# A decoder layer on one core: the last gate summed on VectorE, the indexer issued within the last projection block

## Chip, core and metric

The kernel runs on one core of a Trainium2 chip, in one launch. The metric is the device time in microseconds, as a median over runs. The core's engines are TensorE (PE, its weight loads PEld), VectorE (DVE), ScalarE (ACT), GpSimd (POOL) and SyncE (SP); SyncE issues nearly all DMAs.

## What is computed

One layer for 256 tokens of width 2048, all in float32:

```
ada = silu(c) W_ada + b_ada -> sh1, sc1, gt1, sh2, sc2, gt2     # six vectors of 2048
h = RMSNorm(x) * (1 + sc1) + sh1
q, k, v, qi, ki, wi, p = split(h W_in)
A = attention(q, k, v) over the 64 keys per query with the highest indexer score
    score = sum over 16 heads of relu(qi . ki) * wi, causal
B = causal averages of p over windows 2, 4, 8, 16, minus p, a linear map per group, a scale
x = x + gt1 * (concat(A, B) W_out)
h2 = RMSNorm(x) * (1 + sc2) + sh2
top-1 of 4 expert groups, then top-2 of its 8 experts; SwiGLU experts of width 512
x = x + gt2 * experts(h2)
```

W_ada has 100 MB, the 32 experts 403 MB, W_in 30 MB and W_out 17 MB; every weight is read once.

## The kernel before

The work goes through in this order. `block_ada` and `block_scales` sum the first two modulation vectors, and `project` (line 459) multiplies by W_in, in five blocks of input rows (`BLOCKS`); the loop at line 518 runs over blocks and over the seven parts of the output (`PARTS`). Then come the pooling sums and the map of the pooled channels (lines 536 to 559), `indexer` (line 369: rope, scores, eight rounds of max and match-replace that mark the 64 best keys), `norm_qk`, `attend` (`probs` and `weigh`) and `out_proj` (line 601), once for the pooled half (`mixP`) and once for the attention half (`mixA`). `out_proj` calls a function after each of its four column tiles: `beside_pool` issues indexer, norms and attention there, `route_block` transposes the finished columns and multiplies them by the router's weights. Then the router's choice, and eight groups of four experts: `gather`, `hidden` (w1 and w3), `down` (w2), `combine`.

The other four modulation vectors are summed meanwhile in pieces of 128 input rows, 1 MB each. `fill(n)` issues the next n steps of `fill_steps`: gt1, sc2, sh2, each sixteen pieces on VectorE (line 161: acc = w * s + acc, one instruction of 128 x 2048) and a step that sums acc over the partitions on TensorE. `gate_end` spreads a gate over the partitions with four products; `vec_end` (line 282) turns a vector into columns with sixteen products of one column. gt2 has steps of its own, `gt2_steps`: sixteen pieces on TensorE, each four products side by side in column groups of the array (line 324), then `end`, with four products and four copies (lines 336 and 337). `FILLS` says how many steps stand behind each part of a projection block.

Weights go into rings of buffers: a ring of four for W_in and W_out (`wtile`), a ring of three for the pieces (`FILL_SLOTS`, with a fourth, `LATE_SLOTS`, once the indexer's tile is free). The experts use twelve buffers (`MOE_SLOTS`), and their first thirteen tiles (`FIRST_SLOTS`) are loaded ahead, as buffers of the earlier stages come free. The pieces' buffers are among them.

Each engine takes its instructions in order. That order isn't the order of the code: a scheduler moves instructions when the kernel is built, as far as dependences and buffers allow.

Of the kernel before, what the change touches and what calls it, by code (L numbers as in the profile page):

```python
# [44 lines left out]
C_ID, C_TRI, C_ROPE, C_ROPE2, C_IOTA, C_DG, C_FILL, C_SEL, C_END = 0, 128, 256, 352, 368, 400, 404, 406, 410  # L45
# [4 lines left out]
def shape_constants():  # L50
# [22 lines left out]
    for g in range(4):  # L73
        k[32 * g, C_SEL + g] = 1.0
# [6 lines left out]
def layer_kernel(ctx: ExitStack, tc: tile.TileContext, x, c, w_ada, b_ada, norm1_g, w_in, q_norm_g,  # L81
# [37 lines left out]
    def t2(shape=(P, 512)):  # L119
        return rot.tile(list(shape), F32, tag="t2", name="t2", bufs=4)  # L120
# [162 lines left out]
    def vec_end(acc, bias, gain, name):  # L283
        av = acc.rearrange("p (k q r) -> p k r q", q=P, r=RB)
        pt = bank([P, KC], "fl")
        for k in range(KC):
            nc.tensor.matmul(pt[:, k:k + 1], lhsT=av[:, k // RB, k % RB], rhs=ones[:, 0:1], start=True, stop=True)
        v = one.tile([P, KC], F32, name=name)
        if gain is None:
            nc.vector.tensor_add(v, pt, bias)  # L290
        else:
            nc.vector.scalar_tensor_tensor(v, pt, 1.0, bias, op0=ALU.add, op1=ALU.add)
            nc.vector.tensor_mul(v, v, gain)
        results[name] = v
# [3 lines left out]
    def fill_steps():  # L298
        v2 = lambda j: v2T[:, 4 * j:4 * j + 4].rearrange("p k r -> p (k r)")
        for name, sec in (("gt1", 2), ("sc2T", 4), ("sh2T", 3)):  # L300
            acc = biased(sec)
            yield from ada_pieces(sec, acc, fill_ring)
            if sec == 2:
                yield lambda: gate_end(acc, name)
            elif sec == 4:
                yield lambda: vec_end(acc, v2(2), v2(0), name)
            else:
                yield lambda: vec_end(acc, v2(1), None, name)


    def gt2_steps():
        gb = one.tile([P, 512], F32, tag="V2", name="gb")
        nc.gpsimd.memset(gb, 0.0)
        for g in range(4):
            nc.gpsimd.dma_start(gb[32 * g:32 * g + 1], b_ada[5 * D + g * 512:5 * D + (g + 1) * 512].unsqueeze(0))
        held = {}

        def piece(k):
            if k == 0:
                held["p"] = bank([P, 512], "fl")  # L320
            w = slot([P, D], fill_ring)
            nc.sync.dma_start(w, w_ada[k * P:(k + 1) * P, 5 * D:6 * D])
            for g in range(4):
# [4 lines left out]
        yield from [lambda k=k: piece(k) for k in range(KC)]  # L328

        def end():  # L330
            gs = t2()
            nc.vector.tensor_add(gs, held["p"], gb)
            gt = one.tile([P, D], F32, tag="gate", name="gt2")
            for n in range(4):
                pt = bank([P, 512], "fl")
                nc.tensor.matmul(pt, lhsT=kc[:, C_SEL + n:C_SEL + n + 1].to_broadcast([P, P]), rhs=gs, start=True, stop=True)
                nc.scalar.copy(gt[:, n * 512:(n + 1) * 512], pt)
            results["gt2"] = gt

        yield end  # L340

    steps = fill_steps()
    gates = gt2_steps()

    def fill(n, of=None):
        for _ in range(n):
            step = next(of or steps, None)
            if step is not None:
                step()
# [165 lines left out]

    PARTS = [("pool", 0), ("pool", 1), ("qi", 0), ("kw", 0), ("qkv", 0), ("qkv", 1), ("qkv", 2)]
    FILLS = {2: (0, 0, 1, 0, 1, 0, 1), 3: (0, 0, 1, 0, 1, 1, 1), 4: (2, 2, 2, 0, 2, 1, 1)}
    for b, (k0, nk) in enumerate(BLOCKS):
        block_scales(b)
        for k in range(k0, k0 + nk):  # L520
            h = hcols(k, slice(0, S))
            nc.scalar.activation(h, h, AF.Identity, scale=s1T[:, k:k + 1], bias=sh1T[:, k:k + 1])
        nxt = block_ada(b + 1) if b + 1 < len(BLOCKS) else []
        for pi, part in enumerate(PARTS):
# [11 lines left out]
    wpl = wtile([P, NG, 2, 256])  # L536
    nc.sync.dma_start(wpl, w_pool.rearrange("g (k p) d -> p g k d", p=P))
    mixP = one.tile([P, KC // 2, S], F32, tag="H1", name="mixP")
    wa = one.tile([P, 8, S], F32, tag="N0", name="wa")
    wb = one.tile([P, 8, S], F32, tag="N1", name="wb")  # L540
    src = ppT
    for lv, dst in enumerate((wa, wb, wa, wb)):
        c0, lag = 2 * lv, 1 << lv
        nc.vector.tensor_add(dst[:, c0:8, lag:S], src[:, c0:8, lag:S], src[:, c0:8, 0:S - lag])
        nc.vector.tensor_copy(dst[:, c0:8, 0:lag], src[:, c0:8, 0:lag])
        src = dst
    for g, dst in enumerate((wa, wb, wa, wb)):
        sl = slice(2 * g, 2 * g + 2)
        nc.vector.tensor_mul(dst[:, sl, 0:EDGE], dst[:, sl, 0:EDGE], edge[:, g][:, None, :].to_broadcast([P, 2, EDGE]))
        nc.vector.scalar_tensor_tensor(ppT[:, sl], dst[:, sl], 1.0 / POOL_WINDOWS[g], ppT[:, sl], op0=ALU.mult, op1=ALU.subtract)  # L550
    for g in range(NG):
        py = bank([P, 2, S], "mm")
        for dd in range(2):
            for k in range(2):
                nc.tensor.matmul(py[:, dd], lhsT=wpl[:, g, k, dd * P:(dd + 1) * P], rhs=ppT[:, g * 2 + k],
                                 start=(k == 0), stop=(k == 1))
        for dd in range(2):
            j = g * 2 + dd
            nc.scalar.activation(mixP[:, j], py[:, dd], AF.Copy, scale=plT[:, j:j + 1])
# [40 lines left out]
    def out_proj(mix, k0, label, after=None):  # L600
        for n in range(4):
# [17 lines left out]
            fill(3)  # L619
# [51 lines left out]
    def route_block(n):  # L671
# [265 lines left out]
    fill(100, gates)  # L937
    for q in range(NQ):
        a = hidden(q * QE, xg)
        held = gwT  # L940
# [39 lines left out]
```

## Time and profile before

| | us |
|---|---|
| median of 3 runs | 1446.32 |
| lowest, highest | 1444.52, 1446.98 |
| the profiled execution | 1448.13 |
| its span, first to last instruction | 1446.3 |
| TensorE busy in it | 1176.1 |
| VectorE busy | 415.2 |
| ScalarE busy | 98.2 |

All times of the trace are counted from the start of the span. Busy shares are no measure of what bounds the kernel by themselves: a transfer of 557 MB runs beside everything, and the stages have different limits. So the trace is read by stage below. A row of the timeline has the start, the time that the instructions took from the first to the last, the engine, the line, the operation, the tile that is written and those read, the shapes, the count, and in brackets the idle time ahead of it with what ended it. A float32 matmul of the code is two matmul instructions of the trace.

### The profile page before, as it was taken

Reading aid. Unit: us, or ns where it says so; the run is one execution under the profiler, and the core shown is the slowest. Engines: PE = TensorE matmul, PEld = TensorE weight load, DVE = VectorE, ACT = ScalarE, POOL = GpSimd, SP = SyncE. Lnnn points to the kernel's source line nnn. Section 1 sums busy time; section 2 is a strip of 40 time slices with the busy share of each in tenths; the row PEclk is TensorE's granted clock in tenths of the full one; section 3 lists DMA queues with packets and bytes.
Section 4 is the critical chain, followed back from the end, with each engine's and each line's share of the span. In section 5 each row is a group of like instructions: output and inputs, shape, how many; then the busy total and the mean of one; then the engine's idle time right before and its main releaser. Section 6 shows DMA issues by size and latency. Waiting matters only on the chain. (4 is left out here: it accounts for less than half of the span.)

```text
span 1446.3 us, 13177 instructions
## 1 busy us (share of the span) xinstructions
PE 1176.1 (81%) x5403; PEld 469.8 (32%) x5403; DVE 415.2 (29%) x709; ACT 98.2 (7%) x222; POOL 9.2 (1%) x14
## 2 busy tenths in 40 slices
PE   6889999994999868868878876886886778688666
PEld 4444654543446513213213211321321321132111
DVE  1476668689711401201200120120120012012002
ACT  3200001013521200000000000000000000000000
POOL 1000000000000000000000000000000000000000
PEclk9999999995998899989988998998998999999888
DMA  9999999998985299999999999999999999999997
GB/s 326 362 390 389 391 357 349 382 323 326 385 335 224 114 422 421 421 422 420 421 422 421 421 421 421 422 421 421 420 421 421 421 421 422 421 422 421 420 399 247
DMA packets 125560, 557.02 MB, mean 385 GB/s; under 512 B 15956, under 2 KB 30252, under 8 KB 69944
## 3 DMA queue, kind: packets, MB, share of 16 engines
q1 hardware_dynamic: 123712, 553.94, 95.8%
q10 hardware_dynamic: 1624, 2.18, 0.4%
q8 instruction: 44, 0.72, 0.2%
q14 instruction: 20, 0.16, 0.0%
q0 software_dynamic: 160, 0.02, 0.0%
HBM read 554.00 MB, written 2.10 MB: 384 GB/s over the span
## 5 line engine op out<-in xcount | busy, mean ns | idle before, releaser
L819 PE MATMUL mm<-w,xg 128*32 128x512 f32 x2048 | 395.1, 697 | 150.0 <-DMA w<-in_w_dram 149.9
L819 PEld LDWEIGHTS mm<-w,xg 128*32 128x32 f32 x2048 | 86.0, 124 | 446.0 <-DMA w<-in_w_dram 272.9
L857 PE MATMUL b<-w,t 128*32 128x512 f32 x896 | 194.8, 613 | 37.9 <-DMA w<-in_w_dram 32.4
L799 DVE TENSOR_SCALAR xg<-b,sc2T,sh2T 128x128 f32<-128x128 f32 x128 | 42.3, 404 | 464.6 <-PE b L795 464.6
L482 PE MATMUL mm<-w,hT 128*128 128x512 f32 (+1 forms) x320 | 128.8, 555 | 12.1 <-DMA w<-in_w_in_dram 10.1
L161 DVE SCALAR_TENSOR_TENSOR acc<-w,sT,acc 128x2048 f32<-128x2048 f32 x48 | 112.6, 2346 | 0.5 <-DMA w<-in_w_ada_dram 0.3
L857 PEld LDWEIGHTS b<-w,t 128*32 128x32 f32 x896 | 48.2, 111 | 179.8 <-issue 87.2
L838 DVE TENSOR_TENSOR t<-b,gt 128x512 f32<-128x512 f32 (+1 forms) x33 | 20.9, 671 | 244.0 <-PE b L857 218.8
L482 PEld LDWEIGHTS mm<-w,hT 128*128 128x128 f32 x320 | 57.7, 200 | 77.7 <-issue 66.2
L823 ACT ACTIVATE t<-mm 128x512 f32<-128x512 f32 x8 | 4.8, 597 | 897.3 <-PE mm L819 897.3
L795 PEld LDWEIGHTS b<-gq,x1c 128*128 128x128 f32 x512 | 60.7, 198 | 15.0 <-issue 10.1
L841 PE MATMUL mm<-t,gwT 128*128 128x512 f32 (+1 forms) x132 | 64.1, 618 | 1.5 <-DVE t L838 1.1
L795 PE MATMUL b<-gq,x1c 128*128 128x128 f32 x512 | 63.9, 285 | 1.2 <-DVE gq L785 1.2
L202 DVE SCALAR_TENSOR_TENSOR bacc<-w,sT,bacc 128x1024 f32<-128x1024 f32 x45 | 57.8, 1284 | 21.7 <-DMA w<-in_w_ada_dram 20.4
L611 PE MATMUL mm<-w,mixA 128*128 128x512 f32 x128 | 60.6, 620 | 1.8 <-ACT mixA L597 1.8
L492 PE MATMUL b<-hT,w 128*128 128x256 f32 x256 | 58.9, 388 | 1.9 <-DMA w<-in_w_in_dram 1.8
L611 PE MATMUL mm<-w,mixP 128*128 128x512 f32 x128 | 56.3, 595 | 0.0
L492 PEld LDWEIGHTS b<-hT,w 128*128 128x128 f32 x256 | 49.6, 195 | 14.0 <-issue 3.9
L843 DVE TENSOR_TENSOR xs<-xs,mm 128x512 f32<-128x512 f32 (+1 forms) x66 | 44.2, 670 | 21.1 <-PE mm L841 20.9
L841 PEld LDWEIGHTS mm<-t,gwT 128*128 128x128 f32 x132 | 21.8, 193 | 43.4 <-DVE xs L843 27.5
L611 PEld LDWEIGHTS mm<-w,mixA 128*128 128x128 f32 x128 | 24.2, 197 | 31.1 <-issue 28.0
L611 PEld LDWEIGHTS mm<-w,mixP 128*128 128x128 f32 x128 | 23.9, 190 | 29.0 <-issue 28.2
(211 smaller groups left out, 542.9 us busy)
## 6 DMA issues: line engine op xcount, KB each, us to landing
w<-in_w_dram SPq DMA_DIRECT2D x380, 1024.0 KB, 19.8
w<-in_w_ada_dram SPq DMA_DIRECT2D x64, 1024.0 KB, 7.5
w<-in_w_ada_dram SPq DMA_DIRECT2D x64, 512.0 KB, 9.4
w<-in_w_in_dram SPq DMA_DIRECT2D x21, 1024.0 KB, 10.5
w<-in_w_out_dram SPq DMA_DIRECT2D x16, 1024.0 KB, 7.0
w<-in_w_in_dram SPq DMA_DIRECT2D x14, 512.0 KB, 9.8
w<-in_w_dram SPq DMA_DIRECT2D x8, 512.0 KB, 12.7
xs<-in_x_dram SPq DMA_DIRECT2D x2, 1024.0 KB, 6.8
```

The costliest lines, as they stand in the source:

```text
L161: nc.vector.scalar_tensor_tensor(acc, w, sT[:, k:k + 1], acc, op0=ALU.mult, op1=ALU.add)
L202: nc.vector.scalar_tensor_tensor(acc, w[:, kk], sT[:, k:k + 1], acc, op0=ALU.mult, op1=ALU.add)
L482: nc.tensor.matmul(po[:, :width], lhsT=hcols(k0 + j, slice(i * P, (i + 1) * P)), rhs=w[:, j], start=(j == 0), stop=(j == nk - 1))
L492: nc.tensor.matmul(ppool[n][:, u], lhsT=w[:, j, u * P:(u + 1) * P], rhs=hcols(k, slice(0, S)), start=(k == 0 and u % 2 == 0), stop=(k == K ...
L611: nc.tensor.matmul(po, lhsT=mix[:, k, i * P:(i + 1) * P], rhs=ws[k // 4][:, k % 4], start=(k == 0), stop=(k == 7))
L795: nc.tensor.matmul(px[:, u], lhsT=x1c[i][:, k // RB, k % RB], rhs=gq[:, i].rearrange("p e s -> p (e s)"), start=(i == 0), stop=(i == NT - 1))
L799: nc.vector.tensor_scalar(xg[:, k], px[:, u], sc2T[:, k:k + 1], sh2T[:, k:k + 1], op0=ALU.mult, op1=ALU.add)
L819: nc.tensor.matmul(h[e * CAP:(e + 1) * CAP, :], lhsT=xg[:, k, e * CAP:(e + 1) * CAP], rhs=ws[e][:, r], start=(k == 0), stop=(k == KC - 1), ...
L838: nc.vector.tensor_mul(y[:, 0:m], py, gt2[:, c0:c0 + m])
L841: nc.tensor.matmul(pz[:, 0:m], lhsT=gwT[:, i], rhs=y[:, 0:m], start=True, stop=True)
L843: nc.vector.tensor_add(xv, xv, pz[:, 0:m])
L857: nc.tensor.matmul(py[n // 2][e * CAP:(e + 1) * CAP, (n % 2) * 512:(n % 2 + 1) * 512], lhsT=aT[:, f, e * CAP:(e + 1) * CAP], rhs=ws[e][:, ...
```

## The change

gt2 becomes the fourth entry of `fill_steps`, with the same sixteen pieces on VectorE and `gate_end`; `gt2_steps` and its constants go. `vec_end` sums acc with four products in column groups, copies the result on ScalarE, transposes it in four steps, and reads one column in 32. `FILLS` puts no step in block 2 and more in block 4. In the last block `indexer` and the pooling sums are issued after the part "kw"; norms stand ahead of the pooled output projection, and all of `attend` behind its first column tile. The steps behind the column tiles are 4, 4, 4, 4 in the pooled half and 9, 9 in the attention half, and what is left (six pieces and `gate_end`) stands behind the first group's `hidden`.

```diff
     def vec_end(acc, bias, gain, name):
-        av = acc.rearrange("p (k q r) -> p k r q", q=P, r=RB)
-        pt = bank([P, KC], "fl")
-        for k in range(KC):
-            nc.tensor.matmul(pt[:, k:k + 1], lhsT=av[:, k // RB, k % RB], rhs=ones[:, 0:1], start=True, stop=True)
+
+        pg = bank([P, 512], "fl")
+        for n in range(4):
+            nc.tensor.matmul(pg[32 * n:32 * (n + 1)], lhsT=ones[:, 0:32], rhs=acc[:, n * 512:(n + 1) * 512],
+                             start=True, stop=True, skip_group_check=True, tile_position=(0, 32 * n))
+        gs = t2()
+        nc.scalar.copy(gs, pg)
+        pt = bank([P, RB, P], "fl")
+        for q in range(RB):
+            nc.tensor.transpose(pt[:, q], gs.rearrange("p (q r) -> p r q", r=RB)[:, q], ident)
+        sums = pt.rearrange("p r (k m) -> p k r m", m=32)[:, :, :, 0]
...
-        for name, sec in (("gt1", 2), ("sc2T", 4), ("sh2T", 3)):
+        for name, sec in (("gt1", 2), ("sc2T", 4), ("sh2T", 3), ("gt2", 5)):
             acc = biased(sec)
             yield from ada_pieces(sec, acc, fill_ring)
-            if sec == 2:
+            if sec in (2, 5):
                 yield lambda: gate_end(acc, name)
...
-    def gt2_steps():
...
-            for g in range(4):
-                nc.tensor.matmul(held["p"][32 * g:32 * (g + 1)], lhsT=sT[:, k:k + 1].to_broadcast([P, 32]),
-                                 rhs=w[:, g * 512:(g + 1) * 512], start=(k == 0), stop=(k == KC - 1),
-                                 skip_group_check=True, tile_position=(0, 32 * g))
...
+    def pool_sums():
...
+    def pool_map():
...
-    FILLS = {2: (0, 0, 1, 0, 1, 0, 1), 3: (0, 0, 1, 0, 1, 1, 1), 4: (2, 2, 2, 0, 2, 1, 1)}
+    FILLS = {3: (0, 0, 0, 0, 1, 1, 1), 4: (4, 4, 4, 3, 3, 3, 3)}
...
+            if last and part[0] == "kw":
+                indexer()
+                pool_sums()
...
+    mixP = pool_map()
...
             if after is not None:
                 after(n)
-            fill(3)
...
-    stages = [indexer, norm_qk, attend]
-
     def beside_pool(n):
-        if n < len(stages):
-            stages[n]()
+        if n == 0:
+            attend()
+            fill_ring[:] = LATE_SLOTS
+        fill(4)
 
     while "gt1" not in results:
         fill(1)
+    norm_qk()
     out_proj(mixP, 8, "wo_pool", beside_pool)
-    fill(14)
-    fill_ring[:] = LATE_SLOTS
...
-        if n < 3:
-            while n >= 1 and "sh2T" not in results:
-                fill(1)
-            if n == 2:
-                route_bias()
-            fill(6, gates)
+        if n < 2:
+            fill(9)
+        if n == 2:
+            route_bias()
...
     xg, gwT = gather(0)
-    fill(100, gates)
     for q in range(NQ):
         a = hidden(q * QE, xg)
+        if q == 0:
+            fill(100)
```

`pool_sums` and `pool_map` hold the pooling lines as they stood, in two functions.

The orders show three places. On VectorE, from the last sums of the projection (`pqkv`) on: `score` is the indexer's, `t` and `xs` belong to the pooled output projection. Before:

```order
L477 TENSOR_TENSOR pqkv<-pqkv,mm 128x512 x2
L161 SCALAR_TENSOR_TENSOR acc<-w,sT,acc 128x2048 x3
L615 TENSOR_TENSOR t_1074<-mm,gt_988 128x512
L616 TENSOR_TENSOR xs<-xs,t_1074 128x512
L161 SCALAR_TENSOR_TENSOR acc<-w,sT,acc 128x2048
L615 TENSOR_TENSOR t_1086<-mm,gt_988 128x512
L381 COPY t_1107<-pidx 128x128
```

And in the changed kernel:

```order
L386 TENSOR_SCALAR score<-r_1003,wis 128x128
L450 TENSOR_TENSOR pqkv<-pqkv,mm 128x512
L388 SCALAR_TENSOR_TENSOR score<-r_1003,wis,score 128x128
L159 SCALAR_TENSOR_TENSOR acc<-w,sT,acc 128x2048
L388 SCALAR_TENSOR_TENSOR score<-r_1003,wis,score 128x128
L450 TENSOR_TENSOR pqkv<-pqkv,mm 128x512
L388 SCALAR_TENSOR_TENSOR score<-r_1003,wis,score 128x128
```

The scores now begin among the projection's last sums; before, eight output products of the pooled half (`t`, `xs`) began ahead of them.

On TensorE, in the third column tile of the attention output projection (`mixA`); `fl` is written by the modulation sums, `sm` by the router's products. Before:

```order
L676 MATMUL b_1955<-kc,xs 128x128 x4
L324 MATMUL fl<-w,sT 32x512 x16
L611 MATMUL mm<-w,mixA 128x512 x2
L676 MATMUL b_1955<-kc,xs 128x128 x4
L611 MATMUL mm<-w,mixA 128x512 x6
L287 MATMUL fl<-ones,acc 128x1 x16
L683 MATMUL sm<-ws_1692,r_1964 128x36 x8
L611 MATMUL mm<-w,mixA 128x512 x3
L336 MATMUL fl<-t_2025,kc 128x512
```

And in the changed kernel, where the vector's sum stands a column tile earlier:

```order
L593 MATMUL mm<-w,mixA 128x512 x14
L285 MATMUL fl<-acc,ones 32x512 x4
L593 MATMUL mm<-w,mixA 128x512 x10
L656 MATMUL b_1719<-kc,xs 128x128 x4
L291 MATMUL fl<-kc,t_1773 128x128 x4
L593 MATMUL mm<-w,mixA 128x512
```

The gate's pieces (L324) and its spreading (L336) are gone from here, and the sixteen one-column products (L287) have become L285 and L291.

On SyncE, the first group's weights (L792 up, L831 down) with the six late pieces (L158), in the changed kernel; before, this stretch held expert tiles alone:

```order
L792 DMA w<-in_w_dram 128x2048 x8
L158 DMA w<-in_w_ada_dram 128x2048
L792 DMA w<-in_w_dram 128x2048 x11
L831 DMA w<-in_w_dram 128x2048
L158 DMA w<-in_w_ada_dram 128x2048 x3
L831 DMA w<-in_w_dram 128x2048 x8
L158 DMA w<-in_w_ada_dram 128x2048 x2
L831 DMA w<-in_w_dram 128x2048 x7
```

On VectorE five of the six sums follow in a row there, where before nothing stood between the first group's product and the second group's input (`xg`):

```order
L802 TENSOR_TENSOR t_2316<-t_2316,mm 128x512
L782 COPY gwT<-sm 128x256
L159 SCALAR_TENSOR_TENSOR acc<-w,sT,acc 128x2048
L810 COPY t_2417<-sm 128x512
L159 SCALAR_TENSOR_TENSOR acc<-w,sT,acc 128x2048 x5
L777 TENSOR_SCALAR xg<-b_2357,sc2T,sh2T 128x128 x8
L777 TENSOR_SCALAR xg<-b_2382,sc2T,sh2T 128x128 x8
```

So the second group's input has moved behind the last of the late pieces.

## Rows read from the trace of the kernel before

**Rows 1.** The page, 40 slices of 36.2 us: busy tenths of DMA, and GB/s.

```profile
DMA  9999999998985299999999999999999999999997
GB/s 326 362 390 389 391 357 349 382 323 326 385 335 224 114 422 421 421 422 420 421 422 421 421 421 421 422 421 421 420 421 421 421 421 422 421 422 421 420 399 247
```

**Rows 2.** Stages: length, busy us (count) by engine, clock, DMA share, GB/s.

```profile
0.00:221.70 221.70, 194.76 (x714) 112.47 (x715) 120.54 (x125) 26.55 (x42) 4.95 (x8) 0.96 1.01 366
221.70:262.00 40.30, 40.30 (x126) 19.70 (x127) 35.05 (x55) 4.36 (x9) 1.81 (x1) 1.00 0.95 364
262.00:382.70 120.70, 99.75 (x376) 55.27 (x374) 99.88 (x184) 34.73 (x119) 2.44 (x5) 0.86 0.92 348
382.70:496.50 113.80, 107.92 (x460) 65.33 (x460) 33.45 (x78) 27.74 (x47) 0.00 (x0) 0.91 0.64 250
496.50:501.00 4.50, 4.50 (x45) 1.46 (x48) 4.12 (x13) 0.00 (x0) 0.00 (x0) 1.00 0.01 4
501.00:1446.30 945.30, 728.87 (x3692) 215.55 (x3682) 122.18 (x258) 4.78 (x8) 0.00 (x0) 0.92 1.00 413
```

**Rows 3.** VectorE: first pooling sum, last softmax reciprocal, the page's group of piece sums.

```profile
221.72 2.28 DVE L544 TENSOR_TENSOR wa<-ppT 128x2040 f32<-128x2040 f32 x1 [6.50 <-ACT ppT L495]
...
382.56 0.17 DVE L581 RECIPROCAL sm<-sm 128x4 f32<-128x4 f32 x1
...
L161 DVE SCALAR_TENSOR_TENSOR acc<-w,sT,acc 128x2048 f32<-128x2048 f32 x48 | 112.6, 2346 | 0.5 <-DMA w<-in_w_ada_dram 0.3
```

**Rows 4.** VectorE's waits, 221.7 to 382.7: total us, times, longest.

```profile
DVE t L615 <- PE mm L611: 11.7, 4, 6.0
...
DVE pqkv L477 <- PE mm L482: 5.2, 4, 2.7
...
DVE r L573 <- PE b L570: 3.0, 2, 1.6
```

**Rows 5.** TensorE's timeline after 382.7, and the first expert product.

```profile
389.09 9.68 PE L611 MATMUL mm<-w,mixA 128*128 128x512 f32 x22
...
401.75 2.78 PE L324 MATMUL fl<-w,sT 128*32 128x512 f32 x24
...
433.31 1.87 PE L683 MATMUL sm<-ws,r 128*128 128x36 f32 x16
...
437.38 3.64 PE L324 MATMUL fl<-w,sT 128*32 128x512 f32 x32
...
448.39 7.40 PE L287 MATMUL fl<-ones,acc 128*128 128x1 f32 x32
455.65 3.61 PE L683 MATMUL sm<-ws,r 128*128 128x36 f32 x16
459.06 5.35 PE L611 MATMUL mm<-w,mixA 128*128 128x512 f32 x6
464.25 1.02 PE L336 MATMUL fl<-t,kc 128*128 128x512 f32 x2
...
496.51 12.29 PE L819 MATMUL mm<-w,xg 128*32 128x512 f32 x102
```

**Rows 6.** Windows of 4 us, columns as in rows 2.

```profile
452.00:456.00 4.00, 4.00 (x19) 4.00 (x18) 0.17 (x1) 0.00 (x0) 0.00 (x0) 0.74 0.01 4
...
460.00:464.00 4.00, 4.00 (x6) 1.69 (x5) 0.00 (x0) 0.00 (x0) 0.00 (x0) 0.50 0.00 0
...
480.00:484.00 4.00, 0.82 (x4) 0.85 (x5) 2.58 (x18) 2.41 (x4) 0.00 (x0) 0.65 0.00 0
484.00:488.00 4.00, 2.80 (x13) 2.67 (x14) 1.96 (x10) 0.07 (x1) 0.00 (x0) 0.50 0.02 4
```

**Rows 7.** TensorE and VectorE from the first group's up products to its down products.

```profile
545.96 1.04 PE L819 MATMUL mm<-w,xg 128*32 128x512 f32 x2 [1.35 <-DMA w<-in_w_dram]
...
561.70 6.71 PE L857 MATMUL b<-w,t 128*32 128x512 f32 x40 [0.78 <-DVE t L832]
...
551.03 2.64 DVE L799 TENSOR_SCALAR xg<-b,sc2T,sh2T 128x128 f32<-128x128 f32 x8 [50.34 <-PE b L795]
```

More of the change, by code (lines that the diff above doesn't have):

```diff
@@ L283, in vec_end @@
     def vec_end(acc, bias, gain, name):
[L284 to L287 removed]
+        pg = bank([P, 512], "fl")
[8 more added lines that the diff above has]
+        sums = pt.rearrange("p r (k m) -> p k r m", m=32)[:, :, :, 0]
         v = one.tile([P, KC], F32, name=name)
+        vv = v.rearrange("p (k r) -> p k r", r=RB)
         if gain is None:
[L290 removed]
+            nc.vector.tensor_add(vv, sums, bias)
         else:
[L292 to L293 removed]
+            nc.vector.scalar_tensor_tensor(vv, sums, 1.0, bias, op0=ALU.add, op1=ALU.add)
+            nc.vector.tensor_mul(vv, vv, gain)
         results[name] = v
@@ L308, in fill_steps, with fill @@
                 yield lambda: vec_end(acc, v2(1), None, name)
-    def gt2_steps():
[L312 to L323, printed above, removed]
-                nc.tensor.matmul(held["p"][32 * g:32 * (g + 1)], lhsT=sT[:, k:k + 1].to_broadcast([P, 32]),
-                                 rhs=w[:, g * 512:(g + 1) * 512], start=(k == 0), stop=(k == KC - 1),
-                                 skip_group_check=True, tile_position=(0, 32 * g))
[L328 to L340, printed above, removed]
     steps = fill_steps()
-    gates = gt2_steps()
-    def fill(n, of=None):
+    def fill(n):
         for _ in range(n):
-            step = next(of or steps, None)
+            step = next(steps, None)
             if step is not None:
@@ L514, in project @@
                 plain(pidx[:, i, 1024:1104], w, 80, i)
+    def pool_sums():
+        wa = one.tile([P, 8, S], F32, tag="N0", name="wa")
+        wb = one.tile([P, 8, S], F32, tag="N1", name="wb")
+        src = ppT
+        for lv, dst in enumerate((wa, wb, wa, wb)):
+            c0, lag = 2 * lv, 1 << lv
+            nc.vector.tensor_add(dst[:, c0:8, lag:S], src[:, c0:8, lag:S], src[:, c0:8, 0:S - lag])
+            nc.vector.tensor_copy(dst[:, c0:8, 0:lag], src[:, c0:8, 0:lag])
+            src = dst
+        for g, dst in enumerate((wa, wb, wa, wb)):
+            sl = slice(2 * g, 2 * g + 2)
+            nc.vector.tensor_mul(dst[:, sl, 0:EDGE], dst[:, sl, 0:EDGE], edge[:, g][:, None, :].to_broadcast([P, 2, EDGE]))
+            nc.vector.scalar_tensor_tensor(ppT[:, sl], dst[:, sl], 1.0 / POOL_WINDOWS[g], ppT[:, sl], op0=ALU.mult, op1=ALU.subtract)
+    def pool_map():
+        wpl = wtile([P, NG, 2, 256])
+        nc.sync.dma_start(wpl, w_pool.rearrange("g (k p) d -> p g k d", p=P))
+        mixP = one.tile([P, KC // 2, S], F32, tag="H1", name="mixP")
+        for g in range(NG):
+            py = bank([P, 2, S], "mm")
+            for dd in range(2):
+                for k in range(2):
+                    nc.tensor.matmul(py[:, dd], lhsT=wpl[:, g, k, dd * P:(dd + 1) * P], rhs=ppT[:, g * 2 + k],
+                                     start=(k == 0), stop=(k == 1))
+            for dd in range(2):
+                j = g * 2 + dd
+                nc.scalar.activation(mixP[:, j], py[:, dd], AF.Copy, scale=plT[:, j:j + 1])
+        return mixP
     PARTS = [("pool", 0), ("pool", 1), ("qi", 0), ("kw", 0), ("qkv", 0), ("qkv", 1), ("qkv", 2)]
-    FILLS = {2: (0, 0, 1, 0, 1, 0, 1), 3: (0, 0, 1, 0, 1, 1, 1), 4: (2, 2, 2, 0, 2, 1, 1)}
+    FILLS = {3: (0, 0, 0, 0, 1, 1, 1), 4: (4, 4, 4, 3, 3, 3, 3)}
     for b, (k0, nk) in enumerate(BLOCKS):
@@ L523, in layer_kernel @@
         nxt = block_ada(b + 1) if b + 1 < len(BLOCKS) else []
+        last = b + 1 == len(BLOCKS)
         for pi, part in enumerate(PARTS):
@@ L533, in layer_kernel @@
             piece()
[L536 to L559, printed above, removed]
+    mixP = pool_map()
     REP = NH // NKV
```

5 lines of the change are left out of this document (2 added, 3 removed).

## The prediction

> **What bounds the kernel now.** I read the slices first [rows 1]: the DMA engines are 90% busy or more in most slices and move 420 GB/s from slice 15 to the end, but slices 11 to 14 sink to 114 GB/s. The table by stage [rows 2] puts a figure on it. From 501 us on the transfers run at a share of 1.00 for 945.3 us: the expert weights are the bound there, and nothing but bytes shortens that stage. Between 382.7 and 496.5 the share is 0.64, and from 496.5 to 501 it is 0.01. So the time is the moment at which expert weights begin to flow without a pause, plus the 945.3 us that they then need. That moment is set by the first expert product: it starts at 496.51 [rows 5], and only its reads free the buffers that already hold weights. What sets the end is therefore the chain up to 496.51, not the transfers.
>
> That chain has two halves. Up to 382.7 VectorE leads: it does the pooling, the top-64 search, the norms, the softmax, and the running sums of the modulation pieces, and the last softmax reciprocal comes at 382.56 [rows 3]. It is busy 35.05 of the 40.3 us from 221.7 and 99.88 of the next 120.7 [rows 2]: 134.9 of 161.0 us. From 382.7 TensorE leads, busy 107.9 of 113.8 us [rows 2]: the attention half of the output projection, the router, the gather.
>
> **The change part by part.**
>
> *Indexer and attention earlier.* VectorE's order holds the same operations between the first pooling sum and the last softmax reciprocal, except that 28 running sums stand there in place of 29. The work is thus 134.9 minus one sum of 2.35 [rows 3], 132.6 us; with no idle time at all the mark would come at 221.7 + 132.6 = 354. Of the 26.1 us of idle time, 11.7 are waits for products of the pooled output projection [rows 4]: VectorE then has nothing else queued. In the new order scoring, search and norms stand between these, so I let them go. The waits for the last projection products (5.2) and for the attention scores (3.0) [rows 4] have no new cover; I keep these 8 us. The mark falls at 362, 20.7 us earlier. The ends are 354 (no idle) and 376 (all but 4 us of the idle time stays). I take 362 because the largest wait is the one whose place is filled. The projection before it doesn't move: on SyncE's queue 20 modulation pieces stand ahead of the last projection weight in both orders, and the scoring products that TensorE now does among the projection's are moved, not added. The memset and bias load that GpSimd gains run beside all this, far from any wait.
>
> *Last gate on VectorE instead of TensorE.* It takes sixteen steps of four column-group products off TensorE. Ten of these lie after 382.7, in four runs of 80 instructions, the first 24 in 2.78 us and the last 32 in 3.64 [rows 5]; with the two between (1.06 and 1.92) 9.4 us, on a stretch where TensorE is full. Of the four products that spread the gate, the first stands in that stretch (1.02 us [rows 5]) and three among the router's last steps, where I credit 1 us: 2 in all. On VectorE ten of the sixteen sums now come before the experts, 10 x 2.35 = 23.5 us; they go behind the mark of 362, where VectorE is busy only 33.45 of 113.8 us [rows 2]. If that cover were gone they would cost their 23.5.
>
> *Vectors summed in column groups.* Sixteen one-column products (32 instructions, 7.40 us at 448.39 [rows 5]) become four column-group products and four transposes. At 24 in 2.78 the first are 0.93 us for eight instructions; the transposes are at most 0.44 each (22 instructions in 9.68 [rows 5]): under 2.7 together. The ScalarE copy between lies behind other products. I take 5.5 saved, between 4.7 and 6. [...] The router products there take 3.61 us where the same sixteen took 1.87, and six instructions take 5.35 where 0.44 each would give 2.6 [rows 5]: 1.7 + 2.7 = 4.4 us. I expect them back.
>
> [...]
>
> *The stretch after the mark.* It was 113.8 us. Less 9.4, 2, 5.5 and 4.4 it is 92.5. Against that, TensorE in the new order has only eight attention output products ahead of the last softmax; before, 22 instructions of them (9.68 us at 389.09) bridged the wait for ScalarE's scaling and copies. I add 5 us of waiting, take off 3.5 for the four products more that are already done (8 x 0.44), and add 3 for a half clock after the pause, as it is seen at 480 to 488 after one [rows 6]. The stretch is 97 us, between 93 (no wait, no half clock) and 103 (twice of both). The first expert product then starts at 362 + 97 = 459, 37.5 us earlier.
>
> *Late pieces.* Six of the gate's pieces now load among the first experts. Each is 1.05 MB; at 421 GB/s [rows 1] that is 2.49 us, 14.9 together, added to the 945.3. Besides, VectorE's order puts five of these sums ahead of the second group's gathered input, and TensorE's order puts the gate's products ahead of the first down projection. Before, that went without a pause: last tile's product at 545.96, down projection at 561.70 [rows 7]. Now the last piece is fourteen tiles behind the last up-projection tile, about 35 us. Behind it come the sum (2.35) and the two conversions (2.64 each [rows 7]): 7.6 us in which three tiles still load. Then the first four tiles must be read, 32 instructions at 6.71/40 us [rows 7], 5.4, before a buffer comes free, and the next load takes up to a tile's 2.49 to run. The transfers pause for about 7.6 + 5.4 + 2.5 - 7.5 = 8 us, from 0 (the order of landing is kinder) to 14 (half clock).
>
> **The sum.** -20.7 (mark) - 16.8 (stretch) + 14.9 (bytes) + 8 (pause) = -14.6 us. The profiled execution took 1448.13 us with a span of 1446.3, so it is 1.8 over the median of 1446.32; I take the difference from the trace and apply it to the median: 1432.
>
> **The rivals.**
>
> *VectorE's chain does not come earlier (slower).* VectorE takes its queue in order, and 28 sums of 2.35 us, 66 of the 132.6 us, stand inside the chain of scores, search and softmax. Each must wait for its own megabyte, in a ring of three buffers, and the output weights share the queue. If the pieces land late, the mark stays at 382.7: 20.7 us are gone and the bytes and the pause remain, 1432 + 20.7 = 1452. It decides from a mark at 376.5. For it speaks that VectorE has only 26.1 us of idle time before the mark, less than the search and the sums can be shifted about in. Against it: all 48 sums together waited 0.5 us, 0.3 of them for DMA [rows 3].
>
> *The gain is larger.* No idle time before the mark (354), a stretch of 94 us, and no pause: -28.7 - 19.8 + 14.9 = -33.6, 1413. For it: VectorE's waits have single causes [rows 4]. Against it: the products that feed it are themselves in a full TensorE queue.
>
> *The late pieces hold the experts up.* The two last pieces need buffers that come free only after sums that stand behind the first group's own product. If that puts the pieces one behind the other, the pause is about 20 instead of 8: 1444, no change to be told.
>
> *The half clock stays.* If it is not the one-column products that bring it but the short router products around them, which the change keeps, the 4.4 us stay: 1436. For it speaks that the router's own products run in the same windows; against it, that the clock was still full where such products ran alone (1.87 us for sixteen at 433.31 [rows 5]). [...]
>
> **How the numbers follow.** Forecast 1432: 0.50. Larger gain, 1413: 0.20. Half clock stays, 1436: 0.06. Late pieces, 1444: 0.12, a third of it still below the bound. VectorE's chain, 1452: 0.12. What a measurement of this kernel can tell from no change is 0.2%, 2.9 us, so faster is below 1443.4: 0.50 + 0.20 + 0.06 + 0.04 = 0.80; the same 0.08; slower 0.12. The range goes from 1414, at the larger gain, to 1446, which leaves out the slower case and the best tail.
>
> **What would show it.** In the changed kernel the last softmax reciprocal should stand near 362 and the first expert product near 459; the DMA share should be near 0 for some 15 us before the experts instead of 20, and dip once for 5 to 10 us at the first down projection; no half clock behind the vector sums; from there a share of 1.00 for about 960 us. The forecast is wrong in its first step if the mark stands later than 370, in its second if the first expert product is more than 103 us behind the mark, in its third if the experts' stage is longer than 945.3 + 15 + 14.

## The result

The changed kernel takes 1425.84 us (median of four runs, 1424.56 to 1427.49) where the kernel before took 1446.17 beside it: a ratio of 0.9861 (0.9844 to 0.9879), 20.3 us less. The forecast was 1432. In the two profiled executions the difference is larger, 1448.13 to 1424.56, 23.6 us, because the one of before lies 2.0 above its median and the one of after 1.3 below its own. The sum of the steps is held against these 23.6.

The slices of the changed kernel's page (35.6 us each), to be laid beside [rows 1]: one slice is weak, the 13th, where the 13th and 14th were, and a new dent stands in the 16th.

```profile
DMA  9999998999992998999999999999999999999998
GB/s 325 357 386 387 399 373 339 357 369 366 375 385 113 422 422 335 421 422 421 422 422 421 421 422 421 421 421 421 422 420 422 421 421 422 421 421 421 420 405 282
```

The stages, cut at the same marks as in [rows 2]: first pooling sum, last softmax reciprocal, first expert product, transfers running again. The columns are those of [rows 2].

```profile
222.93:262.00 39.07, 39.07 (x137) 18.62 (x138) 35.63 (x65) 5.98 (x13) 1.81 (x1) 1.00 0.92 344
262.00:359.67 97.67, 90.67 (x296) 46.74 (x294) 95.60 (x174) 32.91 (x111) 2.29 (x2) 0.98 0.97 368
359.67:452.10 92.43, 86.41 (x353) 55.28 (x353) 54.20 (x85) 26.09 (x46) 0.00 (x0) 0.89 0.74 295
452.10:457.00 4.90, 4.90 (x49) 1.58 (x52) 4.11 (x13) 0.00 (x0) 0.00 (x0) 1.00 0.17 25
457.00:1422.70 965.70, 724.92 (x3698) 213.79 (x3686) 136.04 (x264) 8.41 (x13) 0.00 (x0) 0.92 1.00 412
```

VectorE is now busy 131.2 of the 136.7 us up to the mark, where it was busy 134.9 of 161.0. The mark, and VectorE's waits up to it (total, times, longest), which answer [rows 3] and [rows 4]:

```profile
359.67 0.18 DVE L563 RECIPROCAL sm<-sm 128x4 f32<-128x4 f32 x1 [0.71 <-ACT r L562]
```

```profile
DVE wa L496 <- ACT ppT L468: 4.1, 1, 4.1
DVE kiT L358 <- PE sm L357: 2.9, 1, 2.9
DVE sm L563 <- ACT r L562: 1.5, 2, 0.8
DVE pqkv L450 <- PE mm L455: 0.3, 1, 0.3
```

The first of these waits lies just ahead of the first pooling sum, so outside the stretch. Of the 11.7 us for pooled output products nothing is left.

TensorE behind the mark, as in [rows 5] (L573 turns the attention weights, L593 is the output projection, L285 and L291 the vector's sum, L647 the router's bias, L663 the router, L797 the experts):

```profile
360.08 4.24 PE L573 MATMUL b<-kc,r 128*128 128x128 f32 x16 [2.58 <-ACT r L565]
...
380.67 1.06 PE L285 MATMUL fl<-acc,ones 128*32 128x512 f32 x8
381.67 8.85 PE L593 MATMUL mm<-w,mixA 128*128 128x512 f32 x20
...
390.82 0.65 PE L291 MATMUL fl<-kc,t 128*128 128x128 f32 x4
...
426.93 4.97 PE L647 MATMUL sm<-wr,sh2T 128*128 128x36 f32 x32
432.28 3.60 PE L663 MATMUL sm<-ws,r 128*128 128x36 f32 x16 [0.38 <-DVE brt L649]
...
452.10 12.01 PE L797 MATMUL mm<-w,xg 128*32 128x512 f32 x102
```

And the dent: windows of 4 us (as in [rows 6]) around the first down projection, then the rows of VectorE, TensorE and SyncE from the timeline that belong to it (as in [rows 7]).

```profile
544.00:548.00 4.00, 1.67 (x2) 0.50 (x2) 3.96 (x7) 0.00 (x0) 0.00 (x0) 0.50 1.01 420
548.00:552.00 4.00, 3.40 (x7) 0.69 (x6) 3.50 (x11) 0.59 (x1) 0.00 (x0) 0.50 0.34 139
552.00:556.00 4.00, 4.00 (x34) 0.99 (x32) 0.00 (x0) 0.59 (x1) 0.00 (x0) 1.00 0.02 4
556.00:560.00 4.00, 4.00 (x34) 1.23 (x34) 0.00 (x0) 0.59 (x1) 0.00 (x0) 1.00 0.90 330
```

```profile
541.44 4.83 DVE L159 SCALAR_TENSOR_TENSOR acc<-w,sT,acc 128x2048 f32<-128x2048 f32 x2 [13.49 <-DMA w<-in_w_ada_dram]
...
546.33 2.08 PE L277 MATMUL fl<-acc,ones 128*128 128x512 f32 x2 [27.56 <-DVE acc L159]
...
521.51 2.81 SPq L158 DMA_DIRECT2D w<-in_w_ada_dram  x2
```

The last two pieces are issued at 521.51, when their buffers come free, and are summed from 541.44; VectorE waits 13.49 us for them and TensorE 27.56 for the sum. By then the expert buffers are full: SyncE waits 11.1 us for a down product before it can issue the next load. From 549 to 556 hardly anything is moved, and 7.0 us are lost in these windows (4 us times what each lacks to 1).

Three terms make the difference between the profiled executions: the mark 382.56 to 359.67, -22.9; mark to first expert product 113.95 to 92.43, -21.5; from there to the end of the span 949.8 to 970.6, +20.8. Together -23.6.

### The profile page after: what moved, and what is told of

It reads as the page before. It is cut to its first block, busy times and chain, and to the rows that moved or that the text cites. A ratio compares the mean times of both kernels' runs of the same rounds, so it can differ in the third digit from the quotient of the medians.

```text
span 1422.7 us, 12863 instructions
## 1 busy us (share of the span) xinstructions
PE 1136.9 (80%) x5235; PEld 446.8 (31%) x5235; DVE 448.2 (32%) x724; ACT 99.9 (7%) x224; POOL 9.0 (1%) x11
## 5 line engine op out<-in xcount | busy, mean ns | idle before, releaser
L797 PE MATMUL mm<-w,xg 128*32 128x512 f32 x2048 | 392.3, 684 | 158.2 <-DMA w<-in_w_dram 158.0
L797 PEld LDWEIGHTS mm<-w,xg 128*32 128x32 f32 x2048 | 84.9, 122 | 449.3 <-DMA w<-in_w_dram 275.8
L835 PE MATMUL b<-w,t 128*32 128x512 f32 x896 | 187.9, 600 | 33.8 <-DMA w<-in_w_dram 28.4
L159 DVE SCALAR_TENSOR_TENSOR acc<-w,sT,acc 128x2048 f32<-128x2048 f32 x64 | 150.2, 2347 | 14.5 <-DMA w<-in_w_ada_dram 13.8
L455 PE MATMUL mm<-w,hT 128*128 128x512 f32 (+1 forms) x320 | 128.9, 555 | 15.2 <-DMA w<-in_w_in_dram 11.6
L773 PEld LDWEIGHTS b<-gq,x1c 128*128 128x128 f32 x512 | 60.2, 196 | 18.1 <-issue 11.7
L593 PE MATMUL mm<-w,mixA 128*128 128x512 f32 x128 | 56.7, 594 | 0.7 <-ACT mixA L579 0.7
L593 PE MATMUL mm<-w,mixP 128*128 128x512 f32 x128 | 56.1, 594 | 0.4 <-DVE t L597 0.4
L802 DVE TENSOR_TENSOR t<-t,mm 128x512 f32<-128x512 f32 x8 | 5.5, 687 | 139.5 <-PE mm L797 139.5
L593 PEld LDWEIGHTS mm<-w,mixP 128*128 128x128 f32 x128 | 24.0, 190 | 29.9 <-issue 27.3
## 6 DMA issues: line engine op xcount, KB each, us to landing
w<-in_w_dram SPq DMA_DIRECT2D x380, 1024.0 KB, 19.8
```

The costliest lines, as they stand in the source:

```text
L159: nc.vector.scalar_tensor_tensor(acc, w, sT[:, k:k + 1], acc, op0=ALU.mult, op1=ALU.add)
L455: nc.tensor.matmul(po[:, :width], lhsT=hcols(k0 + j, slice(i * P, (i + 1) * P)), rhs=w[:, j], start=(j == 0), stop=(j == nk - 1))
L593: nc.tensor.matmul(po, lhsT=mix[:, k, i * P:(i + 1) * P], rhs=ws[k // 4][:, k % 4], start=(k == 0), stop=(k == 7))
L773: nc.tensor.matmul(px[:, u], lhsT=x1c[i][:, k // RB, k % RB], rhs=gq[:, i].rearrange("p e s -> p (e s)"), start=(i == 0), stop=(i == NT - 1))
L797: nc.tensor.matmul(h[e * CAP:(e + 1) * CAP, :], lhsT=xg[:, k, e * CAP:(e + 1) * CAP], rhs=ws[e][:, r], start=(k == 0), stop=(k == KC - 1), ...
L835: nc.tensor.matmul(py[n // 2][e * CAP:(e + 1) * CAP, (n % 2) * 512:(n % 2 + 1) * 512], lhsT=aT[:, f, e * CAP:(e + 1) * CAP], rhs=ws[e][:, ...
```

## The experiments

Each was timed beside the kernel before on its chip (medians of 1444.6 to 1446.9). The table gathers the three marks of every profiled execution; each row's experiment follows. The profiled execution lies 7.6 us above the median in e3, 3.8 in e2 and 1.5 in e5, so the marks of these three rows can't be set against the medians beside them.

| kernel | median us | ratio to before | last softmax reciprocal | first expert product | from it to the end |
|---|---|---|---|---|---|
| before | 1446.17 | 1 | 382.56 | 496.51 | 949.8 |
| changed | 1425.84 | 0.9861 (0.9844 to 0.9879) | 359.67 | 452.10 | 970.6 |
| e1 | 1476.07 | 1.021 (1.0191 to 1.0228) | 412.25 | 498.20 | 974.8 |
| e2 | 1438.74 | 0.9944 (0.9926 to 0.9962) | 366.61 | 467.25 | 973.6 |
| e3 | 1439.95 | 0.9957 (0.9942 to 0.9973) | 358.53 | 460.84 | 984.8 |
| e4 | 1407.01 | 0.9721 (0.9703 to 0.9739) | 359.81 | 455.87 | 950.8 |
| e5 | 1461.63 | 1.0087 (1.0059 to 1.0114) | 365.03 | 476.17 | 985.1 |
| e6 | 1426.59 | 0.9868 (0.9853 to 0.9883) | 358.12 | 451.89 | 972.9 |
| e7 | 1412.40 | 0.9767 (0.9749 to 0.9785) | 361.27 | 460.19 | 950.1 |
| e8 | 1407.19 | 0.9732 (0.9718 to 0.9745) | 360.48 | 457.17 | 949.9 |
| e9 | 1424.38 | 0.9850 (0.9808 to 0.9892) | 358.31 | 450.91 | 971.2 |
| e10 | 1423.41 | 0.9854 (0.9838 to 0.9871) | 359.39 | 451.71 | 969.6 |

### e1: the move undone

The changed kernel with the indexer, the norms and the attention back beside the pooled output projection.

```diff
-            if last and part[0] == "kw":
-                indexer()
-                pool_sums()
...
+    pool_sums()
     mixP = pool_map()
...
+    stages = [indexer, norm_qk, attend]
     def beside_pool(n):
-        if n == 0:
-            attend()
+        if n < len(stages):
+            stages[n]()
+        if n == 2:
             fill_ring[:] = LATE_SLOTS
         fill(4)
...
-    norm_qk()
```

> The changed kernel with the indexer, the norms, the pooling sums and the attention issued where they stood before; gate and vectors stay as changed. Theory A (forecast's first step: the gain before the last softmax reciprocal comes from the place of the search): the reciprocal goes back from 359.7 to 380 or later, the first expert product from 452 to 472 or later, VectorE again waits some 10 us for pooled output products; 1445 us (1440 to 1452). Rival B (the gate's and the vectors' shorter work on TensorE, or the other placing of the pieces, brings it): the reciprocal stays before 370 and the time is at most 1436.

Measured: 1476.07, with the mark at 412.25, some thirty us beyond A's figure. The group of the running sums between the first pooling sum and the mark tells why, first in e1, then in the changed kernel (columns as in the last row of [rows 3]); behind them VectorE's wait for pooled output products in e1.

```profile
L159 DVE SCALAR_TENSOR_TENSOR acc<-w,sT,acc 128x2048 f32<-128x2048 f32 x42 | 98.3, 2342 | 0.1
```

```profile
L159 DVE SCALAR_TENSOR_TENSOR acc<-w,sT,acc 128x2048 f32<-128x2048 f32 x29 | 68.0, 2346 | 0.0
```

```profile
DVE t L595 <- PE mm L591: 13.2, 4, 6.0
```

The window of the changed kernel ends at 359.9, and the last of its 29 sums starts behind the mark:

```profile
359.76 9.48 DVE L159 SCALAR_TENSOR_TENSOR acc<-w,sT,acc 128x2048 f32<-128x2048 f32 x4
```

So 42 sums stand ahead of the softmax in e1 and 28 in the changed kernel. The scheduler put fourteen more into VectorE's queue (that it did so because nothing else was ready there is not shown), and they cost 14 x 2.34 = 32.8 of the 52.6 us. The other 19.8 go with the wait for output products, which is back (13.2; before 11.7). Beside the kernel before, which has 29 sums there, e1 has thirteen more, and 382.56 + 13 x 2.34 = 413.0 is its mark within 1 us. So A is right about the direction and B falls, but the move is worth more in company: with a gate of sixteen more sums on VectorE, it is also what keeps these out of the softmax's way. Its price of 20 by itself is worked out here; e5 measures it.

### e2: the vectors summed as before

`vec_end` of the kernel before, with its sixteen one-column products, in the changed kernel.

```diff
-        pg = bank([P, 512], "fl")
-        for n in range(4):
-            nc.tensor.matmul(pg[32 * n:32 * (n + 1)], lhsT=ones[:, 0:32], rhs=acc[:, n * 512:(n + 1) * 512],
...
+        pt = bank([P, KC], "fl")
+        for k in range(KC):
+            nc.tensor.matmul(pt[:, k:k + 1], lhsT=av[:, k // RB, k % RB], rhs=ones[:, 0:1], start=True, stop=True)
```

> The changed kernel with the one-column products of before in vec_end. Theory A (work and clock): two times 7.4 us in place of 1.7, one of them behind the softmax, and half clock behind it that slows the next products by up to 4.4: the first expert product moves from 452.1 to 460 (458 to 463), the time from 1425.8 to 1434. Rival B (work alone, the clock falls later anyhow, in the router's last products): 457.8 and 1431.5. Rival C (the vector sums are off the path): 1426.

Measured: 1438.74, 12.9 more than the changed kernel, and more than any of the three expected. The first expert product is 15.2 us later, in two parts. The mark is 6.9 later, which none of the theories had: the first vector's sum stands ahead of it, VectorE's idle time up to it is 4.2 longer, and one running sum more (2.3) stands there too, so not all of the 6.9 is shown to be the vector's. The stretch behind it is 8.2 longer, as A says. TensorE's rows there (L285 is here the one-column product, L585 the output projection) and windows of 6 us, columns as in [rows 2]:

```profile
385.23 4.13 PE L285 MATMUL fl<-ones,acc 128*128 128x1 f32 x18
389.22 5.38 PE L585 MATMUL mm<-w,mixA 128*128 128x512 f32 x8
394.43 3.20 PE L285 MATMUL fl<-ones,acc 128*128 128x1 f32 x14
397.49 10.07 PE L585 MATMUL mm<-w,mixA 128*128 128x512 f32 x16
```

```profile
390.00:396.00 6.00, 6.00 (x15) 3.34 (x14) 1.33 (x3) 0.00 (x0) 0.00 (x0) 0.73 0.73 268
396.00:402.00 6.00, 6.00 (x13) 3.40 (x14) 5.86 (x6) 1.86 (x4) 0.00 (x0) 0.55 0.95 359
```

The one-column products take 7.3 us instead of 1.7, and the wide products behind them 0.67 and 0.63 us each, where 20 took 8.85 in the changed kernel (0.44): 1.8 + 3.0 us, at a granted clock of 0.73 and 0.55 in windows that show TensorE busy throughout (6.00 of 6.00 us). In the changed kernel the same place runs at full clock (granted clock 1.00 from 380 to 392). So the granted clock fell in both kernels that have the one-column products here (to 0.74 and 0.50 before [rows 6], to 0.73 and 0.55 in e2) and not in the one without them: in this case they bring it down.

### e3: the gate on TensorE

`gt2_steps` of the kernel before, behind the other fill steps.

```diff
-        for name, sec in (("gt1", 2), ("sc2T", 4), ("sh2T", 3), ("gt2", 5)):
+        for name, sec in (("gt1", 2), ("sc2T", 4), ("sh2T", 3)):
...
+    def gt2_steps():
...
+    def all_steps():
+        yield from fill_steps()
+        yield from gt2_steps()
-    steps = fill_steps()
+    steps = all_steps()
```

> The changed kernel with gt2 summed on TensorE as before, six pieces still loaded among the first experts. Theory A: ten pieces and their part of TensorE's queue cost 9.4 us again in the stretch behind the softmax, while the pause of the transfers at the first down projection (7 us) shrinks, since no running sums stand ahead of the gate's products: first expert product at 461, then 963 us, time 1428 (1424 to 1434). Rival B (the pause comes from the pieces' late landing, not from VectorE's sums): the pause stays 5 us or more and the time is 1434 or more.

Measured: 1439.95. The stretch is 102.3 instead of 92.4, 9.9 longer, as both theories have it. The pause does not shrink, it grows: the experts' part takes 984.8 instead of 970.6. TensorE waits for a late piece, and three windows of 6 us show the transfers stopped:

```profile
550.23 1.93 PE L331 MATMUL fl<-w,sT 128*32 128x512 f32 x8 [21.33 <-DMA w<-in_w_ada_dram]
```

```profile
560.00:566.00 6.00, 6.00 (x40) 5.30 (x40) 1.78 (x6) 0.59 (x1) 0.00 (x0) 0.87 0.00 0
566.00:572.00 6.00, 4.01 (x26) 2.85 (x24) 3.84 (x12) 1.17 (x2) 0.00 (x0) 0.98 0.00 0
572.00:578.00 6.00, 5.22 (x26) 1.20 (x28) 0.69 (x1) 0.00 (x0) 0.00 (x0) 0.50 0.01 3
```

In TensorE's order the pieces' products stand ahead of the second group's gather here, so it waits 21.33 us with that behind it. B is right: the late landing is what hurts, and with the pieces on TensorE it hurts more than with them on VectorE. How much more is uncertain: if the whole 7.6 us by which the profiled execution lies above the median were in this part, the median would leave 977 of the 984.8.

### e4: the late pieces ahead of the experts

```diff
         if n == 2:
             route_bias()
+            fill(6)
```

> The changed kernel with the six late pieces issued behind the third column tile of the attention half, ahead of the experts; only the gate's four spreading products stay behind the first up projection. Theory A: the DMA engines stand idle from 431 to 457, 25 us, and six pieces need 15, so their bytes and the pause (14.9 + 7) go: first expert product at 452 to 457 (two sums more in the router's chain), then 949, time 1406 (1402 to 1411). Rival B (the pieces take the place of loads that were ahead, and the router's sums wait for them): the first expert product is 8 us or more later and the time is 1415 or more.

Measured: 1407.01, 18.8 below the changed kernel and 40 below the kernel before: A. The stretch behind the mark moves more bytes (first row below; 348 GB/s for 96.06 us against 295 for 92.43, so 6.2 MB more, the six pieces), and where the changed kernel's transfers stood still they run (second row e4, third row the changed kernel):

```profile
359.81:455.87 96.06, 87.08 (x353) 55.50 (x353) 67.31 (x91) 26.27 (x46) 0.00 (x0) 0.88 0.89 348
...
436.00:440.00 4.00, 1.37 (x7) 1.23 (x6) 3.14 (x5) 0.00 (x0) 0.00 (x0) 0.50 0.98 350
```

```profile
436.00:440.00 4.00, 0.45 (x3) 0.48 (x3) 3.49 (x24) 0.47 (x2) 0.00 (x0) 0.50 0.00 0
```

Behind the first expert product 950.8 us are left, as before the change (949.8). The price is 3.8 us at that product: a running sum now stands in the router's chain, and TensorE's wait for the chosen experts grows from 3.67 to 5.81.

### e5: the move alone

e3 and e2 together: the gate on TensorE and the one-column vectors, everything else as changed.

> The move of the indexer and of the attention alone: gt2 on TensorE and the one-column vectors as in the kernel before, the fill steps spread as in the changed kernel (six pieces late). Theory A (the move brings the reciprocal forward by itself, and the three costs add up): last softmax reciprocal at 359 to 367, the stretch 92.4 + 8.2 (e2) + 9.9 (e3) = 110.5, the first expert product at 473 (470 to 478), then 985 as in e3 with its pause of 20: 1460 (1452 to 1465), slower than before. Rival B (the reciprocal comes forward only because TensorE has less to do): reciprocal later than 375, time over 1468.

Measured: 1461.63, slower than before by 0.9% (0.6 to 1.1). The mark is at 365.03, the stretch 111.1, the rest 985.1: A in all three, and the costs add up. So the move, with the new spread of the fill steps, brings the mark forward by 17.5 us, and by itself, with six pieces left for the experts' stage, it loses.

### e6, e9, e10: the pause

Three attempts to take the pause away and leave the pieces' bytes among the experts. In e6 the gate's products wait for the first down projection's result.

```diff
-            fill(100)
+            fill(6)
...
+            nc.tensor.matmul(pt, lhsT=lhs, rhs=acc[:, n * 512:(n + 1) * 512], start=True, stop=True)
...
+        held_py["py"] = py[1][:, 1024 - P:1024]
+        fill(1)
         for n in range(4):
             combine(
```

(`lhs` is a tile of ones, written by VectorE as 0 times the down projection's result plus 1.)

> The changed kernel with the gate's four products behind the first down projection (they wait for its result through a small VectorE operation), the six pieces where they are. It takes the pause alone. Theory A (the products waiting for the last running sum are what holds the down projection): down projection at 518 instead of 549, no pause, bytes of the pieces remain: first expert product at 452, then 963 instead of 970.6: 1419 (1416 to 1421). Rival B (the pause is the pieces' own loads in the queue): 1426.

Measured: 1426.59, as the changed kernel. The gate's products no longer hold anything, and the down projection still starts at 548.85:

```profile
548.85 1.93 PE L841 MATMUL b<-w,t 128*32 128x512 f32 x6 [30.17 <-DVE xg L783]
```

Now it waits for the conversions of the second group's input, which stand behind all six sums, because that input is written into the buffer (`B8`) in which one of the late pieces sits. In e9 the pieces keep out of it:

```diff
+            fill_ring[:] = FILL_SLOTS
             fill(6)
```

> The kernel of e6, and the six late pieces keep to their three own buffers and leave the fourth, in which the second group's gathered input is written. In e6 the down projection waited 30 us for the conversions into that input, which stood behind all six running sums, since the input's buffer still held a late piece. Theory A (the shared buffer is what turns the pieces' late landing into a pause): the conversions come at 510 to 518, the down projection at 521 instead of 549, the transfers do not pause, the stage behind the first expert product takes 963 to 966 instead of 970.6, and the time is 1419 (1416 to 1422). Rival B (the pieces' own queue or the gate's later products hold the experts up): a pause of 5 us or more between 520 and 600, 1425 or more.

Measured: 1424.38, no difference that this can tell: the pause of B, with a time 0.6 below B's bound. The conversions are done by 512.75, the first down products run at 517.65, and then TensorE waits for a tile that comes 5.3 us after SyncE's issue at 540.25; SyncE had waited there until the sum of a late piece was done and its buffer free:

```profile
545.53 3.62 PE L841 MATMUL b<-w,t 128*32 128x512 f32 x4 [24.25 <-DMA w<-in_w_dram]
...
540.25 16.51 SPq L837 DMA_DIRECT2D w<-in_w_dram  x7
```

In e10 the pieces are issued within the first up projection, and their sums stand ahead of its product:

```diff
+            if e0 == 0 and kb == 1:
+                fill(100)
         a = t2()
```

> The changed kernel with the six late pieces and the gate's products issued within the first group's up projection, behind its second round of weights, in place of behind it: their sums then stand ahead of the first group's product on VectorE, which is idle there (60 us without an instruction before 517), and the pieces land and leave their buffers before the down projection. Their bytes still load beside the experts. Theory A (the pause comes from pieces that sit in buffers because their sums stand behind the first group's product): no pause, bytes remain; from the first expert product 963 to 965 to the end in place of 970.6, 1419 (1416 to 1422). Rival B (any piece among the experts costs more than its bytes): 1424 or more. If it were as e4 (950.8 behind the first product), the bytes cost nothing.

Measured: 1423.41 and 969.6 us behind the first expert product: far from A, and 0.6 below the bound of B. The pause has moved to the up projection (windows of 6 us):

```profile
526.00:532.00 6.00, 0.63 (x4) 0.20 (x8) 0.00 (x0) 0.09 (x1) 0.00 (x0) 0.63 0.93 388
532.00:538.00 6.00, 6.00 (x48) 1.55 (x44) 0.00 (x0) 0.00 (x0) 0.00 (x0) 0.80 0.24 59
```

Read off as above, the pause is 7.0 us in the changed kernel, 6.7 in e6, 6.4 in e9 and 5.0 in e10. In e2 it is 8.5 and in e1 11.4, with the pieces as in the changed kernel. Each time the wait that had been named is gone and another has its place. What e6, e9 and e10 share is that a piece takes a buffer of the experts' ring and lands some 20 us after its issue (19.8 in the median of the six in the changed kernel, where the expert tiles take 19.4 in the same stretch, 440 to 560; in e9 three are issued from 517.96 on and their sums start at 537.87), and that TensorE takes the tiles in their order (in e3 it waits 21.33 us for a piece with the gather behind it); e4, e7 and e8, without such pieces, have no pause. That this is the cause is argued from these cases; which buffer sets the length was not settled.

### e7 and e8: the half clock before the experts

e7 is e4 with the router's bias issued behind the second column tile instead of the third; e8 is e4 again on the same chip, with twelve steps behind each of the first two column tiles.

```diff
-        if n == 2:
+        if n == 1:
             route_bias()
+        if n == 2:
             fill(6)
```

> The kernel of e4 with the router's bias products (32 instructions of 36 columns) issued one column tile earlier, among wide products. Theory A (in e4 and in the changed kernel they run in one stretch with the router's last narrow products, and there the clock halves): they take 3.7 instead of 4.9, the last router products 1.9 instead of 3.6, and the first expert product comes 3 to 7 us earlier than in e8: 1401 (1398 to 1404). Rival B (ScalarE's and VectorE's copies set that end): within 2 us of e8, and the last router products stay at 3.6.

> e4 once more on the same chip as e7, the six pieces issued behind the first two column tiles (twelve steps each) instead of the third: the scheduler gives SyncE and VectorE nearly the order of e4. Expected as e4: first expert product at 456, time 1407 (1404 to 1409).

Measured: e8 1407.19, as e4. e7 1412.40, slower than e8 although the bias runs at full clock (3.66 us, granted clock 1.00 from 420 to 428). Its rows:

```profile
422.07 3.66 PE L647 MATMUL sm<-wr,sh2T 128*128 128x36 f32 x32
...
432.81 0.75 PE L656 MATMUL b<-kc,xs 128*128 128x128 f32 x4 [0.93 <-DVE xs L598]
435.08 3.63 PE L663 MATMUL sm<-ws,r 128*128 128x36 f32 x16 [1.53 <-ACT r L658]
...
447.07 0.61 PE L719 MATMUL sm<-mem,kc 128*128 128x32 f32 x2 [8.36 <-DVE mem L715]
```

The bias had filled waits for VectorE's and ScalarE's copies. These are now open (0.93 and 1.53), the last router products take 3.63 all the same, and the scheduler has put further sums into the router's chain (a wait of 8.36, in e8 5.82). A falls. Of B only the router's products come true: the time is not within 2 us of e8 but 5.2 above it, 3.0 of them at the first expert product.

## Why the prediction was right, step by step

**The bound** was read rightly. In every kernel the end follows from the first expert product: 950 us behind it with no pieces left (before, e4, e7, e8), 970 to 975 with six of them on VectorE, 985 with them on TensorE (e3, e5, in the profiled executions).

**The mark** (-20.7 forecast, -22.9 measured). VectorE's idle time fell from 26.1 to 5.5 us. The 11.7 went altogether, as forecast. The 8 that I had kept went too: the waits of 5.2 and 3.0 are down to 0.3 and nothing. What is left is mostly waits that I had put at nothing without a reason, 2.9 for the indexer's keys (`kiT`) and 1.5 in the softmax; that 5.5 lies near 8 is luck. The split was incomplete as well: e5 gives the move 17.5, and e2 adds 6.9 with the old vectors. I had costed only the second of the two vector sums and said nothing of the first, which stands ahead of the mark. The rival "VectorE's chain does not come earlier" is out; e1 shows its mechanism at work in another place, fourteen sums for 33 us.

**The stretch** (-16.8 forecast, -21.5 measured). The ten gate pieces were 9.4, and e3 gets 9.9 back with them. The gate's spreading was taken at 2 and is 4.3: all eight instructions lay in the stretch of before (1.02, 1.10, 1.12 and 1.10 us), and I gave the last three products 1 us. The vectors were taken at 5.5 and are 5.7 (7.40 in [rows 5], now 1.06 + 0.65). The added wait was taken at 5; TensorE's waits for ScalarE went from 1.5 to 2.8. The 3 us of half clock behind that pause are there, as 2.2: sixteen instructions of L573 took 4.24, where eight had taken 1.04 before, at a granted clock of 0.71 from 360 to 362 and 0.50 from 362 to 364. Rows of before for this and for the router (L591 turns the attention weights, L667 is the bias, L683 the router):

```profile
388.22 1.04 PE L591 MATMUL b<-kc,r 128*128 128x128 f32 x8
...
469.51 3.66 PE L667 MATMUL sm<-wr,sh2T 128*128 128x36 f32 x32
...
475.77 2.10 PE L683 MATMUL sm<-ws,r 128*128 128x36 f32 x16
```

**The half clock behind the vector sums** went as forecast for the output products, 2.7 us: the granted clock behind the sums was 0.50 before (460 to 464 [rows 6]) and is 1.00 now (380 to 392), and with the one-column products back, in e2, it is 0.73 and 0.55. The router's part of it did not: its 64 instructions take 9.5 us before and 9.4 now, and the bias takes 4.97 instead of 3.66, since the clock now falls a little later, within the run of 36-column products of L647 and L663 (4.97 and 3.60). So the rival "the half clock stays" was half right: it came behind a run of the router's products as well. The windows of the changed kernel:

```profile
424.00:428.00 4.00, 4.00 (x35) 3.78 (x34) 1.85 (x5) 2.07 (x4) 0.00 (x0) 1.00 0.98 401
428.00:432.00 4.00, 3.90 (x24) 3.76 (x23) 0.92 (x3) 2.90 (x4) 0.00 (x0) 0.64 0.80 334
432.00:436.00 4.00, 3.60 (x16) 3.49 (x16) 0.22 (x2) 0.00 (x0) 0.00 (x0) 0.50 0.00 0
```

**The late pieces** (+14.9 and +8 forecast, +20.8 measured). Size right: e4 takes both away and gets 19.8, and the pause was 7.0. The mechanism was only one of several: in the changed kernel the last sum, the conversions behind it and then the down projection follow one another as I had them, but e6 takes the gate's products and e9 the conversions out of the way without a gain. The condition of the rival with a pause of 20 came true as well: the last two pieces are issued at 521.51, behind the first sum after the first group's product (517.97). Its price was 7.0 here; in e3 22 us are lost (the three windows shown and their neighbours).

All three terms came out better than forecast, by 2.2, 4.7 and 2.1 us; within the stretch the spreading and the wait were mis-sized one way and the half clock the other.

**The idle transfers ahead of the experts** were forecast at 15 us and are 25, from 431 to 457. They were 25 before, too (476 to 501), where I had read 20, and for a shorter gap I gave no working. This was the error that mattered, though not for the time: the loads that can be made ahead had moved forward with the chain, and the gap kept its length. With 25 us the six pieces, 15 us, fit in; the change left them out of it, and e4 puts them there for 18.8 us.

## What to carry to other kernels

Where a stage is bound by its bytes, look for the transfers' idle time just ahead of it and load there what must be loaded at all, as long as its consumer is free then: here that was worth almost as much as the whole change (18.8 us against 20.3). Passengers in a ring of buffers that a stage uses in a fixed order cost more than their bytes here (20.8 us against 14.9), and moving the waits about gained at most 2.4 us. When a chain is taken out of its place, read the order that the scheduler then makes: in e1 it put fourteen sums ahead of the softmax.

## What was not expected of the hardware

TensorE's granted clock fell in stretches that the rows show with no idle time or hardly any: behind 32 products of one column (0.73 and 0.55 in e2, busy 6.00 of 6.00 us in both windows) and within a run of 36-column products (in the changed kernel 0.64 from 428 to 432, busy 3.90 of 4.00, then 0.50 from 432 to 436, busy 3.60 of 4.00). Why an engine shown busy lost it is not shown. Where within a run of narrow products the clock falls is not settled: the same 32 bias instructions took 3.66 us in e7 behind wide products, 4.97 in the changed kernel behind narrow ones, but 3.66 again in e2 behind a like run, where only the 16 behind them were slow (3.36; granted clock 1.00 from 438 to 444, 0.82 from 444 to 450).
